# Two-layer fp32 block on one core: the matmuls that join RWKV's triangular inverse are dealt out in pieces among projection matmuls

## The chip, the cores and the metric

The kernel runs on one core of one Trainium2 chip. The metric is the device time of one execution in microseconds (us), as the median of the runs; lower is better. Engines are named as the profile names them: PE is TensorE (PEld its weight loads), DVE VectorE, ACT ScalarE, POOL GpSimd, SP the engine that issues most DMAs.

## The reference

The input is a sequence of 1024 tokens of width 1024, in fp32. A first block (differential and stick-breaking attention, cross attention to a memory of 256 rows, an MLP of width 4096, RMS norms) is followed by a second, hybrid one. In the second block one projection feeds three mixers (sliding-window attention, RWKV-7 and gated linear attention, GLA), and their outputs go through `w_out`, a gated RMS norm and a residual:

```python
h = _rmsnorm(x, g_pre) * (1.0 + scale[:, None]) + shift[:, None]
proj = h @ w_in
...
def step(S, inp):                                   # RWKV-7, one token
    r_t, w_t, k_t, v_t, kk_t, a_t = inp
    sa = jnp.einsum('bhvk,bhk->bhv', S, -kk_t)
    S = (S * w_t[:, :, None, :] + sa[..., None] * (kk_t * a_t)[:, :, None, :]
         + v_t[..., None] * k_t[:, :, None, :])
    return S, jnp.einsum('bhvk,bhk->bhv', S, r_t)
...
y = jnp.concatenate([attn, rwkv, gla], axis=-1) @ w_out
return x + gate[:, None] * _rmsnorm(y, g_post)
```

The kernel does RWKV's recurrence in chunks of 64 tokens. For each chunk and head the token-by-token correction is a unit lower triangular 64x64 matrix that has to be inverted; there are 32 such matrices (8 chunks of 64 tokens, 4 heads) per half of the sequence.

## The kernel before, in words

The activations stand transposed (features on partitions) and the sequence is worked in two halves of 512 tokens, called chunk 0 and chunk 1 here (`c`). Precision is kept by splitting each fp32 operand into a high and a low part, so that each product is three matmuls (`mm3`, L210, L211, L212). One `mm3` of 128x128 weights on 512 tokens is called a **unit** below. A projection output tile is 8 units (24 matmuls); its weights come by DMA (two of 256 KB), are split by ACT (L202) and POOL (L203) into `wh` tiles, of which there are 8 buffers, and its result leaves PSUM by ACT and DVE (L1586 to L1589, or L2305).

The order of the program's work in the second block is written by a helper, `weave(main, fill, ratio)`. `main` and `fill` are Python generators; each `yield` of `main` names a cost in ns. A positive cost is multiplied by `ratio`, a negative one is taken as it stands, and then `fill` is advanced until the units it emitted (648 each) have paid for that. So `yield 2180` at a ratio of 0.45 brings 981 ns of projections behind that step, and `yield -1000` brings 1000 ns whatever the ratio. The emitted order is a priority: the tile framework's scheduler then places the instructions of each engine by its own model of when each is ready, so the order on an engine follows the emitted one mostly, not always. What it fixes is static: at run time each engine works through its own list in order.

`block2` (L1290) has three such weaves. In the first, `g_rec(0)` (RWKV and GLA of chunk 0) is main and the 13 projection tiles of `g_p2b(0)` with one unit more are fill, 105 units. In the third, `g_rec(1)` and `g_tail` (chunk 1's GLA output and its sliding window, eight units of softmax) are main; the fill is the rest of `g_p2b(1)` (87 units), `g_wout2` (the output projection of chunk 0, 64 units) and `g_wout2a` (the part of chunk 1's output projection that doesn't need the window, 32 units, which can start only when the rows it reads exist).

RWKV's generator `early` in `rwkv` (L1745) runs, for each chunk: four steps `s1` on PE (L1780, L1786) and DVE (L1792); the gate of GLA; four transposes on DVE (L1945); fifteen elimination steps on DVE that invert the 16x16 diagonal blocks (L1955, L1958); transposes back on DVE (L1969, L1978). Then the **join**, which makes 64x64 inverses out of the 16x16 ones with small matmuls:

- 64 matmuls 32x32 on 16 columns (L1986), whose result DVE masks into `Y` (L1988);
- 96 matmuls that need `Y` (L1994, L1997), copied out by ACT and DVE (L1998, L2000);
- two groups of 16 matmuls 32x32 on 32 columns (L2006), each with an ACT copy (L2007), then two more (L2013), each with an ACT copy (L2014).

An fp32 matmul leaves two records in the trace, so these are 128, 192, 64 and 64 records. Behind the join come `s2b` (L1828, ACT L1832), `s2c` (L1842, DVE L1848) and the recurrence over chunks `s3` (L1864, L1869, L1874, L1881, with the state on DVE, L1879), whose steps hang on each other through ACT and DVE copies. GLA and the tail follow.

`g_final0` runs beside `g_wout2a`: it is advanced once for each of the first four units and then after every second unit, 18 times in all, and what is left of it is emitted at the end. It sums the squares of chunk 0's output (four small matmuls, L226), takes the power -1/2 on DVE and POOL (L219, L220), brings the row back by four matmuls (L234) and then finishes chunk 0 row by row (DVE L2344, L2346, POOL L2347).

Of the kernel before, what the change touches and what calls it, by code (L numbers as in the profile page):

```python
# [138 lines left out]
def chain(*gens):  # L139
    for g in gens:  # L140
        yield from g


def weave(main, fill, ratio, flush=True):

    got = 0.0
    for cost in main:
        got += cost * ratio if cost > 0 else -cost  # L150
        while got > 0:
            x = next(fill, None)
            if not x:
                break
            got -= abs(x)
    if flush:
        for _ in fill:
            pass
# [12 lines left out]
class K:  # L171
# [1118 lines left out]
    def block2(s, wp, pre, out):  # L1290
        tc, nc = s.tc, s.nc
        with tc.tile_pool(name="b2", bufs=1, reuse_waits="tile") as b2, tc.tile_pool(name="wk3", bufs=2, reuse_waits="tile") as s.wk, tc.tile_pool(
            name="smC", bufs=4, reuse_waits="tile"
        ) as s.sm:
            s.vt = b2.tile([P, NB, 400], F32, name="vt")
            s.b2_consts(b2)
            with tc.tile_pool(name="lo", bufs=1, reuse_waits="tile") as s.lop:
                with tc.tile_pool(name="wt", bufs=1, reuse_waits="tile") as wt:
                    with tc.tile_pool(name="pp", bufs=2, reuse_waits="tile") as pp:
                        vt = s.vt_load(wt, wp)  # L1300

                        def beside(m):
                            if m == 1:
                                hi = s.tl(s.xp, [P, KT, CH], "act", F32R)
                                lo = s.lop.tile([P, KT, CH], F32R, tag="lo1", name="lo1")
                                s.slow = s.fin_steps(1, hi, lo, s.wk)
                            for _ in range(2 if m >= 2 else 0):
                                next(vt, None)
                            if m == 7:
                                for _ in vt:  # L1310
                                    pass

                        for _ in chain(s.g_p2a(pp, 0, pre, beside), s.g_vt()):
                            pass
                rest = s.g_p2b(1)
                weave(
                    s.g_rec(0), chain(s.g_p2b(0), s.take(rest, s.K0)),
                    0.45
                )
                with tc.tile_pool(name="pp", bufs=2, reuse_waits="tile") as pp:  # L1320
                    weave(
                        s.g_window0(), chain(s.g_p2a(pp, 1), s.take(rest, s.K1)),
                        0.9
                    )
                    while s.steps:
                        s.steps.pop(0)()
                tp = ExitStack()

                def tail():
                    yield from s.g_tail(tp.enter_context(tc.tile_pool(name="tp", bufs=1, reuse_waits="tile")))  # L1330

                main = chain(s.g_rec(1), tail())
                rest = chain(rest, s.g_wout2(b2), s.g_wout2a(s.g_final0(b2, out)))
                weave(main, rest, 0.45, False)
                with tp, tc.tile_pool(name="fp", bufs=1, reuse_waits="tile") as fp:
                    s.finish(fp, wp, out, rest)

# [407 lines left out]
    def rwkv(s, rp, ra, c):  # L1745
# [180 lines left out]
        def early():  # L1926
# [56 lines left out]
            for k in range(32):  # L1983
                for z in range(2):
                    a = slice(32 * z, 32 * z + 32)
                    mm(ps[a, k, :], XU[a, k, 1, a], TD[a, k, :], start=True, stop=True)  # L1986

            V.scalar_tensor_tensor(  # L1988
                Y, ps[0:64], s.m16[0:64, 0:1], s.m16[0:64, None, 1:17].to_broadcast([64, 32, 16]), ALU.mult, ALU.add
            )  # L1990
            yield -2000
            ps, pq = s.ps([P, 32, 16]), s.ps([P, 32, 16])
            for k in range(32):
                mm(pq[0:32, k, :], U[0:32, k, 0:32], Y[0:32, k, :], start=True, stop=True)  # L1994
                for z in range(2):
                    a = slice(32 * z, 32 * z + 32)
                    mm(ps[32 * z : 32 * z + 16, k, :], Y[a, k, :], U[a, k, 32 * z + 16 : 32 * z + 32], start=True, stop=True)  # L1997
            act(TQ[0:32, :, 0:16], pq[0:32], AF.Copy)  # L1998
            for z in range(2):
                V.tensor_copy(U[32 * z : 32 * z + 16, :, 32 * z + 16 : 32 * z + 32], ps[32 * z : 32 * z + 16])  # L2000
            yield 2000
            for g in range(2):
                ps = s.ps([P, 16, 32])
                for i in range(16):
                    k = 16 * g + i
                    mm(ps[32:64, i, :], XU[0:32, k, 1, 32:64], TQ[0:32, k, :], start=True, stop=True)  # L2006
                act(TQ[32:64, 16 * g : 16 * g + 16, :], ps[32:64], AF.Copy)  # L2007
                yield 1000
            for g in range(2):
                ps = s.ps([P, 16, 32])  # L2010
                for i in range(16):
                    k = 16 * g + i
                    mm(ps[0:32, i, :], TQ[32:64, k, :], U[32:64, k, 32:64], start=True, stop=True)  # L2013
                act(U[0:32, 16 * g : 16 * g + 16, 32:64], ps[0:32], AF.Copy)  # L2014
                yield (3860, 1000)[c]

            s2b(0)
            yield (1190, 1744)[c]
# [26 lines left out]
        def late():  # L2045
# [13 lines left out]
            for pr in range(2):  # L2059
                out(pr)  # L2060
                yield 0

        return early(), late()


# [262 lines left out]
    def g_final0(s, b2, out):  # L2328

        nc = s.nc  # L2330
        V = nc.vector
        r = s.sm.tile([P, 4], F32, tag="rz", name=s.nm("rz"))
        yield
        s.rsq(r, s.sums(s.zacc), 1.0 / D, EPS)
        RF = s.rst
        s.bcast(RF, s.rf[:, 0:4])
        yield
        RZ = s.zacc
        s.bcast(RZ, r)
        for mt in range(KT):  # L2340
            h, z = s.tl(s.wk, [P, CH], "t2"), s.tl(s.wk, [P, CH], "t2")
            s.get_rows(h, s.hd, mt, 0)
            s.get_rows(z, s.zd, mt, 0)
            V.scalar_tensor_tensor(h, h, s.gv[:, 4, mt : mt + 1], RF, ALU.mult, ALU.mult)  # L2344
            yield
            V.scalar_tensor_tensor(z, z, s.GP[:, mt : mt + 1], RZ, ALU.mult, ALU.mult)  # L2346
            nc.gpsimd.tensor_tensor(z, z, h, ALU.add)  # L2347
            s.put_rows(out, mt, 0, z)
            yield
# [104 lines left out]
```

## Time and profile before

| | |
|---|---|
| median of 3 runs | 2352.42 us (2352.35 to 4421.85) |
| the profiled execution's own time | 2354.5 us |
| its span, first to last instruction | 2352.7 us |
| mean granted TensorE clock over the span | 0.968 |
| PE busy | 2255.0 us (96%) |
| DVE, ACT, POOL busy | 1251.6, 1035.5, 689.2 us |

The clock is the share of TensorE's full rate that was granted: 1.00 is 2.4 GHz, 0.50 is 1.2 GHz. The profile's second part cuts the span into 40 slices of 58.8 us; a digit is a busy share, or the clock, in tenths. Matmuls are pipelined, so a matmul's duration is longer than the distance from its start to the next one's; prices are read from starts. In a timeline row the bracket tells how long the engine stood idle before, and what ended that; `issue` means that nothing which the profile shows was waited for.

### The profile page before, as it was taken

The page shows a single profiled execution, that of the slowest core. Times are in us where ns is not written, and L with a number is a line of the kernel's source. Part 1 is how long each engine was busy: PE and PEld are TensorE (multiplying, and loading weights), DVE is VectorE, ACT ScalarE, POOL GpSimd, SP SyncE. Part 2 cuts the span into 40 slices and gives each one's busy share as a digit, 9 for nine tenths or more (in the row PEclk, how much of TensorE's full clock was granted, in tenths as well). Part 3 has the DMA queues.
Part 4 walks back from the last instruction along what each step waited for, and adds up shares of the span by engine and source line. Part 5 has one row for each costly group of instructions (what it writes and reads, how often), then busy time and mean ns, then how long its engine had stood idle before and what let it go on. Part 6 is the DMA issues. An engine that isn't in the chain of part 4 may idle for free. (4 is left out here: it accounts for less than half of the span.)

```text
span 2352.7 us, 36021 instructions
## 1 busy us (share of the span) xinstructions
PE 2255.0 (96%) x13696; PEld 1908.1 (81%) x13696; DVE 1251.6 (53%) x2266; ACT 1035.5 (44%) x2198; POOL 689.2 (29%) x1035
## 2 busy tenths in 40 slices
PE   8999999999999999999999999999999998999886
PEld 7898999988898888888888888888787875777765
DVE  7665656676754555423423322346842667526574
ACT  6655656674643424411311312344533357333563
POOL 4101100000500003566666630036321443214443
PEclk9999999999999999999999999999998999969997
DMA  4010010123241211222222211143342333424452
GB/s 135 28 41 23 30 39 28 46 78 122 68 137 54 99 36 50 77 74 79 83 74 79 79 59 51 48 134 121 116 128 76 113 121 118 147 74 134 154 173 75
DMA packets 116541, 200.14 MB, mean 85 GB/s; under 512 B 14192, under 2 KB 33936, under 8 KB 115600
## 3 DMA queue, kind: packets, MB, share of 16 engines
q1 hardware_dynamic: 111600, 184.73, 24.4%
q0 software_dynamic: 4768, 13.11, 1.7%
q8 instruction: 107, 1.75, 0.3%
q14 instruction: 66, 0.54, 0.1%
HBM read 163.71 MB, written 34.08 MB: 84 GB/s over the span
## 5 line engine op out<-in xcount | busy, mean ns | idle before, releaser
L210 PE MATMUL ps<-act,wh 128*128 128x512 f32 x1664 | 667.2, 404 | 8.8 <-ACT wh L202 5.4
L212 PE MATMUL ps<-act,wh 128*128 128x512 f32 x1664 | 658.5, 396 | 0.7 <-POOL wh L203 0.7
L211 PE MATMUL ps<-act,wh 128*128 128x512 f32 x1480 | 583.5, 394 | 3.5 <-DVE act L206 2.5
L202 ACT ACTIVATE wh<-stg 128x512 fp32r<-128x512 f32 x374 | 234.5, 629 | 579.6 <-PE ps L211 467.1
L210 PEld LDWEIGHTS ps<-act,wh 128*128 128x128 f32 x1664 | 317.5, 191 | 79.4 <-ACT wh L202 5.4
L212 PEld LDWEIGHTS ps<-act,wh 128*128 128x128 f32 x1664 | 317.0, 190 | 70.4 <-POOL wh L203 1.1
L211 PEld LDWEIGHTS ps<-act,wh 128*128 128x128 f32 x1480 | 281.6, 190 | 62.1 <-DVE act L206 3.5
L203 DVE TENSOR_TENSOR wh<-stg,wh 128x512 fp32r<-128x512 f32 x260 | 199.7, 770 | 156.4 <-ACT wh L202 154.4
L203 POOL TENSOR_TENSOR wh<-stg,wh 128x512 fp32r<-128x512 f32 x114 | 159.2, 1402 | 370.7 <-ACT wh L202 342.1
L909 DVE TENSOR_TENSOR act<-ps,act 128x512 f32<-128x512 f32 x112 | 77.0, 689 | 177.8 <-PE ps L212 177.7
L548 DVE TENSOR_TENSOR_SCAN pw<-pw,zero 128x128 f32<-128x128 f32 (+7 forms) x64 | 86.8, 1357 | 85.1 <-POOL pw L544 79.9
L249 POOL TENSOR_TENSOR nacc<-nacc,t 128x512 f32<-128x512 f32 x28 | 38.7, 1382 | 261.0 <-ACT t L248 256.6
L1146 DVE SCALAR_TENSOR_TENSOR t<-ps,Rm 128x512 f32<-128x512 f32 x64 | 44.1, 691 | 126.8 <-PE ps L212 126.1
L946 POOL TENSOR_TENSOR ad<-ad,cb 128x256 f32<-128x256 f32 x96 | 73.8, 769 | 125.7 <-DMA ad<-adaT 122.4
L951 POOL TENSOR_TENSOR ad<-ad 128x128 f32<-128x128 f32 (+5 forms) x288 | 97.7, 339 | 16.8
L210 PE MATMUL ps<-hid,wh 128*128 128x512 f32 x256 | 101.2, 395 | 0.0
L212 PE MATMUL ps<-hid,wh 128*128 128x512 f32 x256 | 101.1, 395 | 0.0
L211 PE MATMUL ps<-hid,wh 128*128 128x512 f32 x256 | 101.0, 394 | 0.0
L1147 ACT ACTIVATE t<-t 128x512 f32<-128x512 f32 x64 | 40.4, 632 | 135.8 <-DVE t L1146 135.8
L210 PE MATMUL ps<-wh,act 128*128 128x256 f32 x320 | 95.3, 298 | 0.0
L212 PE MATMUL ps<-wh,act 128*128 128x256 f32 x320 | 90.8, 284 | 0.0
L211 PE MATMUL ps<-wh,act 128*128 128x256 f32 x320 | 90.5, 283 | 0.0
(522 smaller groups left out, 4664.2 us busy)
## 6 DMA issues: line engine op xcount, KB each, us to landing
stg<-w2f SPq DMA_DIRECT2D x84, 256.0 KB, 2.8
stg<-w_dn SPq DMA_DIRECT2D x80, 256.0 KB, 2.7
stg<-w_up SPq DMA_DIRECT2D x64, 256.0 KB, 2.7
ad<-adaT POOLq DMA_DIRECT2D x96, 128.0 KB, 2.5
stg<-w2o SPq DMA_DIRECT2D x32, 256.0 KB, 2.7
pd<-t SPq DMA_DIRECT2D x30, 256.0 KB, 2.2
t<-yd SPq DMA_DIRECT2D x26, 256.0 KB, 3.5
rkd<-RK SPq DMA_DIRECT2D x4, 1280.0 KB, 5.2
```

Source lines behind the costliest of these rows:

```text
L202: nc.scalar.activation(hi, src, AF.Copy)
L203: (eng or nc.vector).tensor_tensor(lo, src, hi.bitcast(F32), ALU.subtract)
L210: mm(out, lh, rh, start=first, stop=False)
L211: mm(out, lh, rl, start=False, stop=False)
L212: mm(out, ll, rh, start=False, stop=last)
L249: nc.gpsimd.tensor_tensor(acc, acc, t[:, :n], ALU.add)
L548: V.tensor_tensor_scan(m[:, :w][:, ::-1], m[:, :w][:, ::-1], s.zero.to_broadcast([P, w]), 1.0, ALU.mult, ALU.add)
L909: s.nc.vector.tensor_tensor(hh, ps, hh, ALU.add)
L946: tt(t, t, cb[:, 256 * y : 256 * y + 256], ALU.mult)
L951: tt(acc[:, n, z, :] if w == 2 else a, a, b, ALU.add)
L1146: V.scalar_tensor_tensor(t, ps, 0.0, R[:, c * CH : (c + 1) * CH], ALU.max, ALU.mult)
L1147: nc.scalar.activation(t, t, AF.Square)
```

## The change

Three things are edited. In the join, L1986's 64 matmuls and the 96 of L1994 and L1997 are given a yield after every 16 and 24 of them, and all yields of the join become negative, so that they no longer depend on the ratio; those behind L2006 and L2013 are now -1400 each. The ratios of the first and third weave go down from 0.45 to 0.27 and 0.29. In `g_final0` one yield ahead of the sums becomes two, and one between the sums' power and the way back becomes four. No instruction is added or removed; only the order changes.

```diff
                 weave(
                     s.g_rec(0), chain(s.g_p2b(0), s.take(rest, s.K0)),
-                    0.45
+                    0.27
                 )
...
-                weave(main, rest, 0.45, False)
+                weave(main, rest, 0.29, False)
...
                     mm(ps[a, k, :], XU[a, k, 1, a], TD[a, k, :], start=True, stop=True)
+                if k % 8 == 7:
+                    yield -1000
...
-            yield -2000
+            yield -700
...
                     mm(ps[32 * z : 32 * z + 16, k, :], Y[a, k, :], U[a, k, 32 * z + 16 : 32 * z + 32], start=True, stop=True)
+                if k % 8 == 7:
+                    yield -1400
             act(TQ[0:32, :, 0:16], pq[0:32], AF.Copy)
...
-            yield 2000
+            yield -700
+
             for g in range(2):
...
-                yield 1000
+                yield -1400
             for g in range(2):
...
-                yield (3860, 1000)[c]
+                yield -1400
...
         r = s.sm.tile([P, 4], F32, tag="rz", name=s.nm("rz"))
-        yield
+        for _ in range(2):
+            yield
         s.rsq(r, s.sums(s.zacc), 1.0 / D, EPS)
         RF = s.rst
         s.bcast(RF, s.rf[:, 0:4])
-        yield
+        for _ in range(4):
+            yield
         RZ = s.zacc
         s.bcast(RZ, r)
```

## Rows read from the trace of the kernel before

**Rows 1.** The page, parts 1 and 2: PE's share, and clock in 40 slices.
```profile
PE 2255.0 (96%) x13696; PEld 1908.1 (81%) x13696; DVE 1251.6 (53%) x2266; ACT 1035.5 (44%) x2198; POOL 689.2 (29%) x1035
...
PEclk9999999999999999999999999999998999969997
```

**Rows 2.** Windows, chunk 0's join: length, busy (instructions) PE PEld DVE ACT POOL, clock, DMA.
```profile
1761.98:1768.96 6.98, 2.63 (x131) 2.43 (x129) 6.83 (x8) 2.47 (x3) 0.83 (x1) 0.69 0.16 47
1768.96:1774.18 5.22, 5.22 (x192) 5.18 (x192) 0.54 (x1) 0.00 (x0) 0.00 (x0) 0.50 0.14 53
1774.18:1780.86 6.68, 6.68 (x24) 5.09 (x21) 1.36 (x2) 1.22 (x2) 1.18 (x1) 0.69 0.00 0
1780.86:1786.26 5.40, 5.40 (x134) 4.86 (x133) 0.69 (x1) 2.99 (x5) 1.38 (x2) 1.00 0.19 52
1786.26:1800.58 14.32, 14.32 (x154) 11.25 (x151) 2.48 (x9) 4.63 (x8) 1.27 (x1) 1.00 0.50 148
```

**Rows 3.** Windows, chunk 1's join and what follows.
```profile
2045.96:2048.12 2.16, 2.16 (x130) 2.12 (x128) 2.12 (x3) 1.07 (x2) 0.81 (x1) 0.97 0.26 56
2048.12:2055.16 7.04, 7.04 (x28) 5.36 (x24) 2.48 (x3) 0.63 (x1) 1.29 (x1) 0.77 0.22 68
2055.16:2058.72 3.56, 3.56 (x175) 3.45 (x174) 0.00 (x0) 0.63 (x1) 0.00 (x0) 0.93 0.69 226
2058.72:2062.25 3.53, 1.31 (x20) 0.84 (x19) 0.60 (x1) 0.59 (x1) 0.00 (x0) 0.50 0.02 5
2062.25:2069.03 6.78, 6.78 (x130) 6.71 (x129) 2.06 (x4) 3.51 (x6) 1.26 (x1) 0.50 0.32 94
2069.03:2090.00 20.97, 20.97 (x143) 17.05 (x141) 2.47 (x9) 3.98 (x7) 0.00 (x0) 0.53 0.18 59
```

**Rows 4.** Timeline of PE: waits ahead of the joins; start us, us, engine line.
```profile
1762.89 2.40 PE L1986 MATMUL ps<-t,XT 32*32 32x16 f32 x126 [0.68 <-DVE t L1969]
1768.96 0.23 PE L1994 MATMUL ps<-t,act 32*32 32x16 f32 x1 [3.66 <-DVE t L1988]
...
2060.94 0.23 PE L1994 MATMUL ps<-t,act 32*32 32x16 f32 x1 [2.22 <-issue]
```

**Rows 5.** Timeline of PE, a visit of projections between small matmuls.
```profile
1782.99 0.50 PE L212 MATMUL ps<-act,wh 128*128 128x512 f32 x1
1783.33 0.40 PE L210 MATMUL ps<-act,wh 128*128 128x512 f32 x1
1783.57 0.39 PE L211 MATMUL ps<-act,wh 128*128 128x512 f32 x1
...
1784.12 2.21 PE L2013 MATMUL ps<-act 32*32 32x32 f32 x64
```

**Rows 6.** Timeline of DVE, chunk 0: the transposes ahead of `Y`, then `Y`.
```profile
1760.69 2.15 DVE L1969 STREAM_TRANSPOSE t<-act 32x512 f32<-32x512 f32 x2
1762.87 4.18 DVE L1978 STREAM_TRANSPOSE act<-act 32x512 f32<-32x512 f32 x4
...
1768.16 0.74 DVE L1988 SCALAR_TENSOR_TENSOR t<-ps,m 64x512 f32<-64x512 f32 x1
```

**Rows 7.** Timeline of PE, waits in the recurrence, one of chunk 0 and one of chunk 1.
```profile
1804.04 2.18 PE L1828 MATMUL ps<-AV,act 64*64 64x128 f32 x16 [0.74 <-ACT AV L1819]
...
2099.16 1.12 PE L1842 MATMUL ps<-XT,WT 64*64 64x128 f32 x8 [1.68 <-ACT WT L1832]
```

**Rows 8.** Timeline of PE and DVE at the first half's sums and their way back.
```profile
2242.36 1.05 PE L226 MATMUL ps<-ones,zacc 128*128 128x1 f32 x8
2248.74 2.08 PE L234 MATMUL ps<-ident,rz 128*128 128x128 f32 x8 [4.32 <-POOL rz L220]
...
2247.44 0.14 DVE L219 TENSOR_SCALAR rsq<-ps 128x4 f32<-128x4 f32 x1
2248.40 0.75 DVE L2344 SCALAR_TENSOR_TENSOR t<-t,gv,rst 128x512 f32<-128x512 f32 x1
```

**Rows 9.** Windows, the window mixer's last stretch, columns as in Rows 2.
```profile
2262.00:2300.00 38.00, 28.67 (x130) 20.47 (x129) 34.58 (x59) 23.80 (x66) 14.90 (x12) 0.92 0.64 200
```

## The prediction

> **What bounds it now.** I read the page first: PE is busy for 96% of the span and its clock falls below full in late slices [rows 1]. So the end is set by PE's list of work, and a change of order can gain only where PE waits or runs at half rate. The table by windows then shows where that is. In chunk 0's join PE is busy for 2.63 of 6.98 us while it waits, and 11.9 us follow at a clock of 0.50 and 0.69 [rows 2]. In chunk 1's join PE stands for 2.2 of 3.53 us and the clock stays near 0.5 from 2058.72 to 2090.00, over which the recurrence's first stages take 20.97 us against 14.32 in chunk 0 at 1.00 [rows 2, 3]. The timeline names the waits: 0.68 and 3.66 us for DVE in chunk 0, 2.22 us for nothing shown (issue) in chunk 1 [rows 4]. DVE's timeline shows why chunk 0 waits: its transposes run on after the first 64 matmuls are done, and `Y` starts at 1768.16 [rows 6].
>
> **What the order becomes.** I add up the yields by hand. Before the join's first matmul the fill has emitted 37 units in both chunks; after the change 34. Behind the first 64 matmuls and `Y` it is 40 units before, 41 after (both chunks). At the join's end it is 48 and 59 units in chunk 0, 44 and 60 in chunk 1. When GLA's load is reached it is 65 and 70, 63 and 72. So the join gets 11 to 16 units more, the stretch before it loses three, and the recurrence behind it keeps 11 of 17 units in chunk 0 and 12 of 19 in chunk 1. Totals are unchanged; the fill runs dry at the same places.
>
> **Prices.** Big matmuls start 0.23 us apart at full clock, so a unit is 0.70. A visit of projections between small matmuls costs 0.20 beyond that: four took 1.13 us instead of 0.93 [rows 5]. The join has two visits now in chunk 0 and about twelve after, so ten more: 2.0 us lost per chunk, 4.0 in all.
>
> *Chunk 0, waits (4.34 us).* `Y` hangs on DVE's chain, which PE can't hasten except by releasing `s1` earlier: by nothing at least, by the three units at most, 2.1 us. One unit more is done by then, 0.7. So 0.7 to 2.8 of the wait goes; I take the middle, 1.8. The rest reappears wherever those units are missing.
> *Chunk 0, clock.* The 192 records took 5.22 us at 0.50; chunk 1 ran 174 in 3.56, so 192 in 3.9: 1.3 back. The 20 projections behind took 6.68 where 4.8 is their price (20 by 0.23 and a visit): 1.9 back. Sum 3.2, if the clock holds; 0 if it doesn't.
> *Chunk 1, join.* The stretch with the issue wait, 3.53 us, holds 0.8 of work at full clock: 2.7 back. 23 projections took 7.04 instead of 5.5: 1.5. L2006 and L2013 took 6.78, and in chunk 0 5.40 less a visit of 1.13, 4.3: 2.5 [rows 2, 3, 5]. Sum 6.7. An issue wait has no named cause; dealing the small matmuls thins the stream of instructions where it arose, but it may return (2.2 less).
> *Chunk 1, behind the join.* The same stages took 20.97 us with 9 projections and 14.32 with 18 in chunk 0; less nine by 0.23 that is 12.2, so 8.8 are lost to the clock [rows 2, 3]. Between nothing and 8.8 I take three quarters, 6.6: chunk 0 ran these stages at 1.00 with one unit a stage, close to what chunk 1 will have.
> *Behind both joins.* Six or seven units fewer cover the recurrence's waits. Bare ones cost 0.74 and 1.68 us [rows 7]. I price two a chunk at 1.0 and as much again for the clock that falls with them (0.93 to 0.50 in chunk 1 around its wait) with a bit over: 3.5 a chunk, 7.0 in all, between 0 and 15.
> *What else moves.* About two projection tiles end inside the join instead of one. Each brings its evacuation and weight splits into ACT's, DVE's and POOL's lists, and SP's loads and stores with them; ACT and DVE are busy for 2.99 and 0.69 of 5.40 us there [rows 2], and two units (1.4 us) stand between a TQ copy and the matmul that needs it. I price that at nothing; without the cover a 0.6 us copy would show per group, 2.4 a chunk, inside the range.
> *The way back.* PE waits 4.32 us for the power of the sums: DVE reaches it at 2247.44, behind softmax work, though the sums were emitted at 2242.36 [rows 8]. After the change seven units (4.9 us) are emitted between the sums and L234, against one. That covers the wait. But four of the 18 steps then remain for the end, and the last stretch is DVE's: 34.58 busy of 38.00 us [rows 9]. Two rows of four L2344/L2346 at 0.75 put 3.0 us there. So between +6 (the wait, and the 2.08 us of L234 at low clock) and -3; I take +2.5.
>
> **Sum.** Chunk 0: 1.8 + 3.2 - 2.0 = 3.0. Chunk 1: 6.7 + 6.6 - 2.0 = 11.3. Behind: -7.0. Way back: +2.5. Together 9.8 us less. Against the profiled execution's 2354.5 that is 2344.7; the median of the runs lies 2.1 lower, so 2342.6, rounded to 2343. The window's tail begins when PE has finished GLA, so a gain in the join passes on to it.
>
> **A rule weighed.** The clock was 0.97 in the 2.16 us of L1986, 0.77 just behind, and 0.50 to 0.53 from 2062.25 to 2090.00 though PE was never idle there (6.78 of 6.78, 20.97 of 20.97 us busy) [rows 3]. The row says that a busy PE on small matmuls doesn't hold the upper level (2.4 GHz), and that projections among them might. The Trainium skill ("TensorE: Matmul & The Clock Gate", Part 1) has the clock set by how busy PE has recently been, with idle gaps as what loses it. By that alone the 8.8 us could not be there, so this trace speaks against it; it is the third rival all the same.
>
> **Rivals.**
> 1. *The order doesn't change where it counts.* The scheduler moves work by its own model: 126 of 128 records of L1986 ran behind units emitted after them (24 projections in one go before it). If it draws the same units forward in both versions, only the way back moves: 2352.4 - 2.5 = 2350. Chance 0.15.
> 2. *Slower: the recurrence goes short.* Place: `s2b` to `s3` behind both joins. The units that moved into the join are missing there, waits lie bare, and the clock stays low as it did in chunk 1. Price: 8.8 newly in chunk 0, 7.0 for waits, 4.0 for visits, less 4.0 for the waits of the joins, nothing from the clock and nothing from the way back: +15.8, so 2368. It decides when chunk 0's stretch behind the join has a clock under 0.75 and chunk 1's none above 0.53. For it: the waits exist already with more cover. Against: chunk 0 at 1.00 with three projections a stage. Chance 0.12.
> 3. *Only idle time counts for the clock.* Then dealing gains no clock: 1.8 + 2.2 for waits, +2.5, less 4.0 for visits and 7.0 behind: +4.5, so 2357. Chance 0.08.
> 4. *Nothing is lost behind the joins.* The scheduler fills those waits from later tiles, as it does elsewhere: 7.0 and the last quarter of 8.8 more: 2343 - 9.2 = 2333. Chance 0.10.
>
> My forecast has 0.55. Its own range is 2335 to 2351: the way back and chunk 0's wait at their bounds, half of the waits' bound. For 8 in 10 the range takes rivals 1, 3 and 4 and leaves out the second: 2329 to 2358. A time is told from no change here when it differs by over 2%, 47 us. No case comes near that: the ceiling of all losses listed is 24.2 in and behind the joins and 6 at the way back. So faster by over 2% gets 0.02, slower 0.02, within 0.96.
>
> **What would show it.** In the changed profile: L1994 in four runs with projections between; no wait of 3.66 before it in chunk 0 and none of 2.2 in chunk 1; a clock of 0.9 or more in both joins and behind chunk 1's; 13 to 15 us instead of 20.97 for the stages behind chunk 1's join; new waits on L1832 or L1819 of some 2 us a chunk; the 4.32 before L234 gone and up to 3 us more DVE work behind 2262. Wrong would be: the same clock in chunk 1 (steps on the clock), or all of this and the same end, the gain then standing as PE waiting in the window's tail.

## The result, and the profile after

The changed kernel takes **2369.73 us** (median of 11 runs), the kernel before 2352.88 beside it (11 runs): a ratio of 1.0059 [1.0047, 1.0071], 14 us slower by the ratio. The forecast was 2343, 10 us faster. The profiled execution after takes 2369.61 us with a span of 2367.8, so the traces lie 15.1 us of span apart. The page, parts 1 and 2:

```profile
PE 2270.0 (96%) x13696; PEld 1915.4 (81%) x13696; DVE 1244.1 (53%) x2266; ACT 1037.3 (44%) x2198; POOL 688.0 (29%) x1035
...
PEclk9999999999999999999999999999989899989897
```

Span less PE's busy time is 97.8 us, and before 97.7 [rows 1]. So PE stands idle no longer than it did; the same 13696 records keep it busy for 15.0 us more. The table by windows (columns as in rows 2) shows where, in the order of the program: chunk 0's first 64 matmuls and their projections, the 23 projections behind them, the second part, the recurrence behind the join, GLA from its first L2161 to L2210, and the step from GLA's last product to its way out (L2260); then for chunk 1 the second part, the projections behind it, the recurrence behind the join, its last stages, and GLA.

```profile
1761.00:1770.91 9.91, 9.91 (x139) 7.23 (x139) 5.22 (x5) 0.63 (x1) 1.27 (x1) 0.50 0.10 28
1770.91:1779.06 8.15, 8.15 (x24) 6.22 (x23) 1.43 (x2) 3.14 (x4) 1.77 (x2) 0.64 0.19 56
1779.06:1784.12 5.06, 5.06 (x198) 4.53 (x197) 0.00 (x0) 0.00 (x0) 0.78 (x1) 0.95 0.21 71
1798.92:1812.40 13.48, 13.48 (x147) 10.44 (x146) 2.13 (x9) 4.21 (x8) 1.26 (x1) 1.00 0.35 106
1854.65:1892.78 38.13, 36.46 (x340) 29.36 (x340) 27.24 (x58) 10.44 (x21) 12.03 (x11) 0.87 0.38 123
1909.29:1922.11 12.82, 7.00 (x31) 5.36 (x30) 8.67 (x14) 11.11 (x19) 5.06 (x5) 0.93 0.58 205
2073.84:2079.61 5.77, 5.77 (x197) 4.96 (x197) 0.00 (x0) 1.23 (x2) 1.27 (x1) 0.79 0.55 185
2079.61:2086.46 6.85, 6.85 (x23) 5.17 (x20) 2.66 (x4) 2.26 (x4) 1.29 (x1) 0.68 0.16 41
2096.64:2113.00 16.36, 16.36 (x158) 12.48 (x158) 3.46 (x11) 6.40 (x13) 2.47 (x2) 1.00 0.46 140
2127.02:2152.62 25.60, 24.85 (x192) 20.49 (x192) 12.47 (x33) 10.80 (x23) 5.07 (x5) 0.77 0.10 32
2162.43:2209.52 47.09, 36.73 (x349) 29.76 (x349) 34.53 (x69) 20.31 (x40) 14.36 (x14) 0.83 0.42 135
```

The kernel before had these four in the places of the fifth, the sixth and the last two (there GLA's line is L2156 and its way out L2255):

```profile
1847.28:1883.32 36.04, 34.95 (x351) 28.30 (x351) 25.65 (x58) 11.49 (x23) 14.01 (x13) 0.96 0.42 140
1898.32:1907.29 8.97, 8.13 (x36) 6.30 (x35) 6.42 (x9) 8.58 (x15) 5.02 (x5) 1.00 0.84 287
2106.00:2130.91 24.91, 24.91 (x213) 19.91 (x213) 14.09 (x33) 12.32 (x26) 9.69 (x5) 1.00 0.32 89
2140.73:2187.82 47.09, 38.39 (x365) 30.67 (x364) 31.59 (x65) 21.20 (x42) 16.06 (x16) 0.93 0.47 149
```

What was hoped for is there. Chunk 0's second part runs at 0.95 where it ran at 0.50 [rows 2], and the stretch behind chunk 1's join at 1.00 where it ran at 0.53 [rows 3]. What was not priced stands beside it: the first 64 matmuls of chunk 0, 2.40 us in one block before [rows 4], are now spread over 9.91 us at half clock. And later places have lost projections. Chunk 1's last stages have 21 records fewer, yet take longer, at 0.77 in place of 1.00. GLA has 11 and 16 fewer, and its clock falls from 0.96 to 0.87 and from 0.93 to 0.83. In the list of PE's waits GLA has 11.6 us in place of 9.8, and the wait for `go` behind it 5.8 in place of 0.8; first after, then before:

```profile
PE ps L2161 <- DVE act L2173: 11.6, 4, 6.7
...
PE ps L2260 <- ACT go L2255: 5.8, 1, 5.8
```

```profile
PE ps L2156 <- ACT t L248: 6.6, 1, 6.6
PE ps L2156 <- DVE act L2168: 3.2, 2, 2.1
...
PE ps L2255 <- ACT go L2250: 0.8, 1, 0.8
```

Starts of the same record in both traces, less 0.233 us (the distance of two projections) for each projection that stands ahead of it in one trace and not in the other, give the delay **on equal work**:

| point | start before, after | projections ahead | delay on equal work |
|---|---|---|---|
| chunk 0, recurrence begins | 1728.42, 1727.21 | 0 | -1.2 |
| first matmul of the second part | 1768.96, 1779.06 | +17 | +6.1 |
| L1828, behind the join | 1786.26, 1798.92 | +33 | +5.0 |
| chunk 1, recurrence begins | 2010.20, 2028.13 | 0 | +17.9 |
| L1828, behind the join | 2069.03, 2096.64 | +39 | +18.5 |
| fourth `s3` | 2106.00, 2127.02 | +45 | +10.5 |
| sums of chunk 0's output, L226 | 2242.36, 2266.25 | 0 | +23.9 |
| last L1710 of the window | 2308.39, 2323.53 | 0 | +15.1 |

So, in these two executions, 12.9 us are lost between chunk 0's join and chunk 1, 8.0 are gained behind chunk 1's join, 13.4 lost from there to the sums, and 8.8 gained at the end.

### The profile page after: what moved, and what is told of

The parts are those of the page before. It is cut to its first block, busy times and chain, and to the rows that moved or that the text cites. A ratio compares the mean times of both kernels' runs of the same rounds, so it can differ in the third digit from the quotient of the medians.

```text
span 2367.8 us, 36012 instructions
## 1 busy us (share of the span) xinstructions
PE 2270.0 (96%) x13696; PEld 1915.4 (81%) x13696; DVE 1244.1 (53%) x2266; ACT 1037.3 (44%) x2198; POOL 688.0 (29%) x1035
```

## The experiments

Ratios are to the kernel before, run on the same chip beside each kernel, with 95% intervals; 1% is 23.5 us. The runs of the kernel before scatter by some 7 us to either side, those of e3, e5, e8 and e17 by 10 to 13. Each trace is one execution.

**The change in parts.**

`e1_way_back`, only `g_final0`:

```diff
-        yield
+        for _ in range(2):
+            yield
...
-        yield
+        for _ in range(4):
+            yield
```

> The kernel before with the two added waits of g_final0 alone (two steps of the filling list ahead of the sums, four ahead of the second broadcast). Theory P (the place): behind the joins the changed kernel was 23.9 us behind at L226 and 15.1 us at the end, so the way back and the tail gave back about 9 us, and this edit alone keeps most of that: the wait of 4.32 us at L234 is gone or under 1 us, and the time is 4 to 9 us less than before, 2344 to 2349 us. Theory T (the tail's slack): the tail only absorbed what came late anyhow, being bound by VectorE; then this edit alone gives 0 to 2 us less, 2351 to 2353 us, and another wait takes the place of the 4.32 us.

2349.78 us, 0.9975 [0.9964, 0.9986]: 5.9 us less by the ratio, theory P. The 4.32 us of rows 8 are gone. The wait of 1.0 us that is left at L234 is another one, later on, which the kernel before has as well. PE's waits in the last 140 us, before and then here:

```profile
PE ps L234 <- POOL rz L220: 5.4, 2, 4.3
```

```profile
PE ps L234 <- POOL rz L220: 1.0, 1, 1.0
```

`e2_join_and_share`, the change without that edit:

> The changed kernel without the added waits of g_final0. Theory P: the way back's gain is lost and the loss of the joins and their shares stands bare: 2374 to 2380 us. Theory T: the tail absorbs the delay without that edit too, so the time is that of the changed kernel, 2366 to 2371 us.

2376.06 us, 1.0074 [1.0052, 1.0097]. The time lies in theory P's range, but the interval overlaps that of the whole change, so it is e1 that sets the two theories apart. The rest of the change costs 17 us; with the way back the whole costs 14.

`e3_share_alone`, whole joins with smaller shares (`0.45` becomes `0.27` and `0.29`):

> The kernel before with the two smaller shares (0.27, 0.29) alone; the joins stay in whole blocks. Theory D (the dealing costs): the loss of the changed kernel sits in the dealt pieces, whose many visits delay Y in chunk 0 and take units from the late recurrence; with the blocks whole and a smaller share, units are only left over for later, so the time is 2348 to 2356 us. Theory S (the share costs): the recurrence runs short of projections under the smaller share, shows bare waits and low clock, and the left-over units come out at the end of each list: 2365 to 2385 us.

2357.43 us, 1.0018 [1.0001, 1.0035]: 4 us, between the theories and nearer to D. Here 18 projections move from ahead of L1986 to behind it in chunk 0, and the wait of 3.66 us at L1994 is gone by that alone. It is not saved: PE stands for 2.3 us at L1986 (1.5 before) and 1.3 at L1818 ahead of it instead, so that from the recurrence's start to the end of the join it is idle for 4.7 us, and before for 5.1.

`e4_deal_alone`, the pieces at the old shares:

```diff
+                if k % 8 == 7:
+                    yield -1000
...
-            yield -2000
+            yield -700
...
+                if k % 8 == 7:
+                    yield -1400
...
```

> The kernel before with the joins' pieces and their negative yields alone; the shares stay at 0.45. Theory D: the dealt pieces delay Y and hold the clock at half as in the changed kernel, and with the larger share the list is also used up earlier, so the late recurrence of both chunks is barer still: 2372 to 2395 us. Theory S: with the larger share the recurrence is fed as before, and only the pieces' own gain is left: 2340 to 2350 us.

2366.85 us, 1.0049 [1.0032, 1.0065]: 11.5 us, a little under D's range and far from S's. The clock is better than before (0.974 over the span against 0.968), but chunk 0's GLA has 28 records fewer than before and PE waits there:

```profile
1854.47:1897.66 43.19, 33.74 (x323) 27.91 (x322) 24.70 (x55) 9.25 (x19) 9.74 (x10) 0.77 0.29 92
```

**Which chunk, and which piece.**

`e6_chunk0` and `e7_chunk1`, the changed kernel with the new join and share in one chunk, here chunk 0 (the other yields likewise):

```diff
-                weave(main, rest, 0.29, False)
+                weave(main, rest, 0.45, False)
...
-                if k % 8 == 7:
+                if k % 8 == 7 and c == 0:
...
```

> The changed kernel with the dealt join and the smaller share in chunk 0 alone; chunk 1 has the join and the share of before, and the way back is the changed one. On equal work the changed kernel lost about 18 us up to the start of chunk 1's recurrence. Theory G (each chunk loses its own in GLA and behind): chunk 0 alone loses those 13 to 18 us, chunk 1 nothing, the way back gives 5: 2362 to 2368 us. Theory C (the loss of chunk 0 is absorbed, since chunk 1 sets the end): 2347 to 2353 us.

> The changed kernel with the dealt join and the smaller share in chunk 1 alone. On equal work the changed kernel gained about 8 us behind chunk 1's join (clock 1.00 in place of 0.53) and lost about 13 between there and L226. Theory G: both remain, +5 to +7 in chunk 1, -5 by the way back: 2352 to 2358 us. Theory C (chunk 1 sets the end, so its loss counts in full and chunk 0's does not): 2362 to 2369 us.

2370.75 us, 1.0063 [1.0047, 1.0078], and 2353.11 us, 0.9993 [0.998, 1.0006]. Less the way back, chunk 0 alone costs some 20 us, more than G said, and chunk 1 some 4, with a time inside G's range. The two and the way back add up to some 19 us, and the whole costs 14; the intervals allow for that. Chunk 0 carries the loss. That it had no clock to win behind its join [rows 2] fits this, but is not tested by itself.

`e5_first_whole`, the changed kernel with L1986 in one block:

```diff
-                if k % 8 == 7:
-                    yield -1000
...
-            yield -700
+            yield -4700
```

> The changed kernel with the first 64 matmuls (L1986) in one block in both chunks; the 4000 of its four steps are added to the step behind Y, so that the same projections stand between the first matmul and the second part. Theory Y (the pieces delay Y): in the changed kernel the last of these matmuls ended at 1770.91 while DVE's transposes were done at 1766.3, and the clock was 0.50 through all 9.91 us; whole, Y starts 3 to 5 us earlier, the second part follows by that much earlier, and the time is 3 to 7 us under the changed kernel, 2362 to 2367 us. Theory G (the shortage in GLA): what is lost is lost behind the joins, since the same projections are missing there; the time is that of the changed kernel within 2 us, 2367 to 2371 us.

2359.87 us, 1.0019 [1.0002, 1.0036]: 9 us under the changed kernel, theory Y, and more than it said. DVE shows one reason. After the change `Y` (L1990) waited 4.65 us for PE's last piece; whole (`Y` is L1988), it starts right behind the transposes. First the changed kernel, then this one, whose trace is 4.2 us later from the recurrence's start on:

```profile
1760.94 4.22 DVE L1978 STREAM_TRANSPOSE act<-act 32x512 f32<-32x512 f32 x4
1765.20 1.11 DVE L1969 STREAM_TRANSPOSE act<-act 32x512 f32<-32x512 f32 x1
1770.96 0.74 DVE L1990 SCALAR_TENSOR_TENSOR t<-ps,m 64x512 f32<-64x512 f32 x1 [4.65 <-PE ps L1986]
```

```profile
1769.44 1.09 DVE L1969 STREAM_TRANSPOSE act<-act 32x512 f32<-32x512 f32 x1
1770.57 0.74 DVE L1988 SCALAR_TENSOR_TENSOR t<-ps,m 64x512 f32<-64x512 f32 x1
```

On equal work, from the recurrence's start to the end of the join, this trace gains 4.7 us on the changed kernel's in chunk 0 and 2.2 in chunk 1. Against the kernel before 4 us are still lost, and with the way back's 5.9 taken off some 10: the price of all the rest, the early units, the pieces of the second part and the smaller share.

**GLA.**

`e9_gla_short`, the kernel before with GLA alone drawing less:

```diff
-                gla = s._gla(gp, c)
+                up = (0.27 / 0.45, 0.29 / 0.45)[c]
+                gla = (x * up if x > 0 else x for x in s._gla(gp, c))
```

> The kernel before with a smaller share in GLA alone: its steps count 0.6 of what they did (chunk 1: 0.64), so that about 75 and 84 projections stand beside L2156 in place of 87 and 103, as in the changed kernel; joins, early recurrence and way back are those of before. Theory G (GLA needs them): waits for DVE before L2156 and a clock under 0.9 there, in both chunks, 5 to 12 us more: 2358 to 2365 us. Theory N (they are only done a little later, and cover something else): 2350 to 2356 us.

2360.22 us, 1.0021 [1.001, 1.0032]: 5 us, at the low end of G. The wait for `go` behind GLA appears. Beside GLA's L2157 PE is idle for more in chunk 0 (3.2 us, and 1.1 before), but for less in chunk 1 (4.9, and 8.7); the clock under 0.9 came in chunk 1 (0.88) and not in chunk 0 (0.95):

```profile
PE ps L2157 <- DVE act L2169: 8.1, 3, 4.0
PE ps L2256 <- ACT go L2251: 5.9, 1, 5.9
```

`e8_gla_share`, the changed kernel with GLA drawing at the old share (`up = (0.45 / 0.27, 0.45 / 0.29)[c]`):

> The changed kernel with GLA's steps scaled up so that they draw at the old share (0.45) while everything else draws at 0.27 and 0.29. Theory G (what the changed kernel lost behind the joins is the shortage beside L2156): about 87 and 100 projections stand there again, the clock there is back over 0.93, and some 5 us return, as much as the shortage alone cost in the kernel before: 2360 to 2366 us. Theory L (the list is finite: the join has taken the units, so GLA only passes the shortage on): the list of chunk 0 runs out before the outputs of GLA and the wait for go (5.8 us) grows; 2367 to 2375 us.

2367.66 us, 1.0057 [1.0037, 1.0077], theory L by a little. Beside L2161 there are 84 and 93 projections again (75 and 84 after the change, 87 and 103 before), but the list then runs dry earlier: the wait for `go` stays (5.9 us), and PE's idle time over the span grows by 14 us.

`e10_whole_gla_way`, whole joins, smaller shares, the same feeding of GLA, and the new way back:

```diff
-                    0.45
+                    0.27
...
+                up = (0.45 / 0.27, 0.45 / 0.29)[c]
...
+        for _ in range(2):
...
```

> The kernel before with the smaller shares, GLA drawing at the old share, and the changed way back; the joins stay in whole blocks. The smaller share alone took away the wait of 3.66 us before L1994 (18 projections fewer before L1986, so that they stand behind it) and cost in GLA. Theory G: with GLA fed, that gain stays and the cost goes: 2340 to 2346 us. Theory L: the units are missing elsewhere; no better than the way back alone, 2348 to 2355 us.

**2343.42 us, 0.9952 [0.9936, 0.9969]**, theory G: faster than both kernels, and nothing in it is dealt. Chunk 0's GLA runs at full clock with PE never idle, 36.04 us before, 32.42 here (with 348 records in place of 351):

```profile
1840.19:1872.61 32.42, 32.42 (x348) 26.21 (x348) 24.47 (x56) 10.32 (x21) 10.93 (x9) 1.00 0.46 154
```

**Only where the clock was low.** `e12_chunk1_old_share` deals chunk 1's join alone, at the old share; `e13_chunk1_whole_old_share` leaves its first part whole. Both have the new way back.

> Dealt join in chunk 1 alone, both shares at 0.45, changed way back. With both chunks dealt at 0.45, chunk 1 went from 19.7 us behind at its start to 0.6 behind (on equal work) at its last stages and 6.9 at L226. Theory G (the dealing pays where the clock had been low for 30 us, and the list of chunk 1, which goes on with the last projection, can bear it): 2340 to 2347 us, faster than the way back alone (2349.8). Theory P (only the way back counts; the pieces' gain is paid back in GLA and the tail): 2348 to 2355 us.

> The same as the kernel with the dealt join in chunk 1 at the old share, but with the first 64 matmuls in one block (their 4000 added behind Y). In the changed kernel that change gave 9 us over both chunks. Theory Y (the pieces of the first part delay Y, in each chunk): 3 to 5 us under its dealt sister, 2336 to 2344 us. Theory Y0 (only in chunk 0, where the clock was at half through the pieces): the same as its sister within 2 us.

2351.08 us, 0.9985 [0.9975, 0.9994], and 2354.67 us, 1.0002 [0.999, 1.0014]. Theory P: on equal work e12 gains 13.3 us from L1828 behind chunk 1's join to the fourth `s3`, then loses 6.5 in GLA and 6.6 from the sums at L226 to the last L1710. Whole, it is no better, if anything 4 us slower (Y0 had said 2 at most). Its trace does gain 1.9 us on e12's up to the end of chunk 1's join; what takes them back is not shown.

**Units or pieces.** The kernels with and without dealing, e8 and e10, are otherwise the same and 24 us apart. `e14_blocks_many` draws e8's units behind e10's whole blocks; `e15_pieces_few` cuts e10's blocks and draws no more than they did:

```diff
-            yield -2000
+            yield -4700
...
-            yield 2000
+            yield -6300
...
```

```diff
+                if k % 8 == 7:
+                    yield -330
...
-            yield -2000
+            yield -680
...
+                if k % 8 == 7:
+                    yield 500
...
-            yield 2000
```

> The kernel with whole joins, smaller shares, fed GLA and the changed way back (2343.4), but its joins draw as many units as the dealt ones: 4700 behind Y, 6300 behind the second part's block, 1400 per group. Nothing else differs from it, and only the pieces are missing against its dealt sister (2367.7). Theory U (the join spends units of a finite list that are wanted behind it, whatever it is cut into): 2360 to 2368 us. Theory V (the visits between pieces and the delay of Y are what costs): 2343 to 2349 us.

> The kernel with whole joins, smaller shares, fed GLA and the changed way back (2343.4), with both blocks cut into pieces, but drawing in all what its whole blocks drew (2000 over the first part and Y, 2000 times the share over the second). Theory U: the pieces cost only their visits, about 0.2 us each: 2343 to 2348 us. Theory V: most of the 24 us between the dealt and the whole joins is back: 2355 to 2368 us.

2366.57 us, 1.0055 [1.0038, 1.0072], theory U in full; and 2357.52 us, 1.0019 [1.0008, 1.0029], inside V's range. Both theories hold, each in its own run: either alone loses most of the 24 us, so they are not two halves of a sum. The window over the whole span tells the ways apart, for e10, e14 and e15 in turn:

```profile
0.00:2335.30 2335.30, 2243.64 (x13696) 1899.03 (x13696) 1266.22 (x2266) 1033.54 (x2198) 687.99 (x1035) 0.97 0.27 86
```

```profile
0.00:2364.50 2364.50, 2248.14 (x13696) 1898.97 (x13696) 1252.78 (x2266) 1035.83 (x2198) 685.25 (x1035) 0.97 0.26 85
```

```profile
0.00:2360.60 2360.60, 2265.13 (x13696) 1916.88 (x13696) 1267.75 (x2266) 1033.85 (x2198) 685.85 (x1035) 0.96 0.26 85
```

Span less PE's busy time is 91.7, 116.4 and 95.5 us. The units drawn early cost **idle time**: 24.7 of 29.2 us. The cuts cost **busy time** on the same records: 21.5 of 25.3 us. (The profile of e10 is its fastest run, 2337.1, and that of e15 one of its slowest, 2362.35; the medians differ by less.) Of the 24.7 us 8.4 stand in chunk 0 from GLA's first to its way out, 4.6 in chunk 1's GLA, and 8.7 between the sums (L226) and the last L1710. So the early units are missed in the window mixer too and not in GLA alone; that last stretch in e10 and e14:

```profile
2243.11:2283.55 40.44, 33.30 (x158) 24.48 (x157) 29.76 (x51) 25.43 (x68) 17.79 (x14) 0.92 0.49 156
```

```profile
2250.26:2320.11 69.85, 54.09 (x252) 39.34 (x253) 48.97 (x93) 43.24 (x118) 25.42 (x20) 0.90 0.50 162
```

Chunk 1's last stages, 25.60 us at 0.77 in the changed kernel, in e8 and e14:

```profile
2121.78:2142.16 20.38, 19.63 (x193) 16.22 (x192) 12.51 (x34) 10.77 (x23) 6.95 (x5) 1.00 0.14 40
```

```profile
2120.95:2141.32 20.37, 19.62 (x192) 16.20 (x192) 12.19 (x33) 10.68 (x23) 7.88 (x5) 1.00 0.12 37
```

`e16_second_pieces` cuts only the second part (`yield 500`), `e17_first_pieces` only the first (`yield -330`):

> The kernel with whole joins, fed GLA and changed way back (2343.4), with only the second part cut into pieces that draw what its block drew. Theory K (the clock of the stretch behind the join hangs on how the first part is entered and left; cutting it put three projections among its matmuls and the same records behind then took 36.0 us at half clock in place of 22.1): this cut touches nothing before L1994, so 2341 to 2347 us. Theory J (any cut of the small matmuls costs): 2350 to 2358 us.

> The same with only the first 64 matmuls cut into pieces, their units taken from the step behind Y. Theory K: one unit stands among them, the clock falls behind chunk 0's join as with both parts cut, 2353 to 2360 us. Theory J: half of the cuts, so between the two, 2347 to 2353 us. Theory N (nothing but visits): 2342 to 2347 us.

2341.78 us, 0.9943 [0.9928, 0.9958], and 2356.89 us, 1.002 [1.0004, 1.0035]: the times of theory K. But on PE the scheduler left the second part in one block in spite of its yields: projections and small matmuls stand in e16 as they do in e10, and in e17 as in e15. So the two pairs are repeats of one another (2343.42 and 2341.78 us; 2357.52 and 2356.89), e15's cuts are those of the first part alone, and what it costs to cut the second part has not been timed: theory J is not ruled out for it. Between the pairs, in the first part of chunk 0 one unit came between the two halves, and that is all that differs up to the end of its join; in chunk 1 a unit stands otherwise in the first part and around one stage of the recurrence, and one projection in GLA. In each of the next two fences the rows are: L1986 up to the second part; the stretch behind the join up to the first `s3`; the next stages. First e16, then e17.

```profile
1765.33:1774.76 9.43, 9.43 (x145) 7.87 (x145) 5.99 (x6) 0.71 (x2) 1.29 (x1) 0.64 0.07 16
1788.67:1796.94 8.27, 8.27 (x71) 6.56 (x71) 0.82 (x3) 3.00 (x5) 0.39 (x1) 0.94 0.01 2
1796.94:1810.64 13.70, 12.96 (x166) 10.57 (x164) 4.90 (x16) 4.71 (x10) 3.17 (x3) 1.00 0.39 116
```

```profile
1765.00:1776.20 11.20, 11.20 (x144) 8.81 (x144) 5.93 (x6) 0.71 (x2) 1.27 (x1) 0.54 0.09 26
1790.66:1805.13 14.47, 14.47 (x72) 11.31 (x71) 0.82 (x3) 3.00 (x5) 1.26 (x1) 0.50 0.08 26
1805.13:1820.73 15.60, 14.86 (x166) 12.04 (x164) 4.90 (x16) 4.71 (x10) 2.29 (x2) 0.86 0.29 79
```

The stretch in the second row holds the same work in both (71 or 72 records), with PE never idle, and takes 8.27 us at 0.94 or 14.47 at 0.50. One unit of 0.7 us, moved by two microseconds, is worth 6.2 us there and 1.9 in the stages behind. The traces of e10 and e15 agree: 8.42 us at 0.92 and 14.47 at 0.50.

## Why the prediction was wrong

The order changed much as the yields say, so the first rival is out; only the stretches ahead of the joins lost six and five units on PE and not three. Of the waits of rows 4 those of 3.66 and 2.22 us are gone. PE waits more ahead of chunk 0's L1986 instead: from the recurrence's start to the end of the join it is idle for 3.5 us, and before for 5.1. That is 1.6 less, and I had put 1.8. (The ceiling of 24.2 us is added up wrong; the losses listed make 23.0. Nothing hangs on it.) By its own steps, against the delays on equal work:

- **Chunk 0's join, 3.0 less: 6.2 more.** The second part did come back: 5.06 us with four projections and a visit, so 3.9, as put. But the same yields cut the first part, which had been one block ahead of a wait for DVE. I priced its visits at 0.20 and nothing else. PE became the late one: `Y` waited 4.65 us for it, and 23 projections more stood behind. The pieces ran at 0.50 throughout. With the first part whole in both chunks, e5 is 9 us faster, and 4.7 us of that show in its trace at this step.
- **Chunk 1's join, 4.7 less (6.7 for waits and clock against 2.0 for visits): 0.6 more.** The wait went, but the second part, the projections behind it and the groups ran at 0.79, 0.68 and 0.83 and not at full clock.
- **Behind chunk 1's join, 6.6 less: 8.0 less.** Right.
- **Behind both joins, 7.0 more: 26.3 more** (12.9 and 13.4). This is the step that failed; it makes 19 of the 25 us between forecast and result. I counted the missing units, right to within three, and priced them by the waits of the first stages [rows 7]. They were missing further back. In chunk 0, GLA and the step behind it lost 0.6 and 5.0 us to waits; by one minus the clock, 1.4 us of GLA's window were lost before and 5.0 after. In chunk 1 the last stages lost 5.9 us by that measure (0 before) and GLA 8.0 (3.3 before). I took the totals at GLA's load as the end of the matter ("the fill runs dry at the same places") and did not ask which work stands bare when a finite list is spent early. The waits in chunk 0 are the shortage's: from GLA's first to its way out PE is idle for 7.5 us, for 7.4 to 8.4 in e5, e6, e8 and e14, whose joins in chunk 0 draw as many units, for 9.1 in e9, where GLA alone draws less, and for 1.9 in the kernel before. The 5.9 us of chunk 1's last stages are not: e8 and e14 have the same 75 projections there and ran at full clock, 5.2 us faster. e14 shows that spending the list early is enough to cost 24 us against e10, and e8 that feeding GLA afterwards doesn't help. But in both the loss is idle time (18.7 and 14.1 us more than before), and in the changed kernel it is busy time (15.0 us, with idle time the same): they do not show by which way the changed kernel lost.
- **The way back, 2.5 less: 5.9 less by itself** [3.3, 8.5 from e1's interval]. Right in kind and near the bound of 6 that I gave; the DVE work I feared at the end didn't show: behind the last L1710 both traces run for 44.3 us.

The second rival gave 2368 and is nearest, but its place and its test were wrong: chunk 0's stretch behind the join has a clock of 1.00, not under 0.75, and chunk 1's 1.00, not 0.53. The waits came in GLA and behind it. The third rival, only idle time counts for the clock, does not hold in these traces: e16 and e17 have the same waits ahead of chunk 0's join (2.1 and 0.84 us) and in it (0.62), PE is never idle in the stretch behind, and the clocks there are 0.94 and 0.50. By the Trainium skill ("TensorE: Matmul & The Clock Gate", Part 1) the clock follows from how busy PE has recently been; in these rows PE's busy share is 100% on both sides.

What stays open is why the clock falls in the one and holds in the other. The runs show one thing that tips it, not the rule; in chunk 1's last stages they do not show even that. Nor is it shown how the 26.3 us divide between fewer projections and a clock that would have fallen anyhow: e9 prices a shortage in GLA alone at 5 us.

## What to carry to other kernels

Filler work in a static order is a finite list: before moving units into one place, name the places that they leave, as far back as the list reaches, and price those by their own waits. A block whose result another engine needs isn't cut while that engine would be ready at its end; here the kernels with the first part whole were 9 us (e5) and 15 us (e16) faster than those with it cut. Edits that come in one change should be timed one by one: the way back gave 5.9 us, feeding GLA and a smaller share about 5 more, and the dealing for which all of it was done took more than both.

## What the hardware showed unasked

The same records in the same order, on a PE that was never idle, ran for 8.27 us at 0.94 or for 14.47 at 0.50, after joins that differ by the place of three matmuls. Each was seen in two traces, and the medians of the kernels (2341.78 and 2356.89 us) lie apart the same way; whether every execution runs like its trace is not shown. Chunk 1's last stages took 25.60 us at 0.77 after the change and 20.4 at 1.00 in e8 and e14, with PE idle for 0.75 us in each. With 32x32 and 64x64 matmuls the clock can stay low for long: in e17 0.50 over all of that stretch, and in chunk 1 of e10, the fastest profile of all, 0.50 over 16.04 us behind the join:

```profile
2061.77:2077.81 16.04, 16.04 (x75) 12.14 (x74) 1.86 (x7) 2.99 (x5) 0.00 (x0) 0.50 0.11 33
```
